# Weight halves kept in DRAM between passes and made beside the first MLP, and indexer scores over two PSUM tags

## The chip, the cores and the metric

One core of a Trainium2 chip runs the whole program. The metric is device time in microseconds (us), from the start of an execution to its end; lower is better. The engines are TensorE (PE, matmuls; PEld its weight loads), VectorE (DVE), ScalarE (ACT), GpSimd (POOL) and SyncE (SP), which here issues the DMA transfers.

## The reference, cut to what matters

Two layers over 1024 tokens of width 1024, in float32:

```python
for i in range(2):
    y = _even_mixer(h, ...) if i == 0 else _odd_mixer(h, positions, ...)
    h = _layer_norm(DN_ALPHA * h + y, ln1_g[i], ln1_b[i])
    u = square(relu(h @ mlp_w1[i])) @ mlp_w2[i]            # 1024 -> 4096 -> 1024
    h = _layer_norm(DN_ALPHA * h + u, ln2_g[i], ln2_b[i])
    h = h + sigmoid(h @ ple_gate_w[i]) * (p[i] @ ple_w[i])
```

The even mixer projects h with one matrix into an mLSTM (chunks of 64, a causal convolution on q and k) and into sparse attention with a compressed, a selected and a windowed branch. The odd mixer projects h to cq (512), ckv (256), a rope key and an indexer key, and then selects keys for each query:

```python
qi  = rope(cq @ w_iq)                                       # 8 indexer heads of 64
isc = einsum('bqh,bqhs->bqs', wi, relu(einsum('bqhd,bsd->bqhs', qi, ki)))
isc = where(causal, isc, NEG);  _, idx = lax.top_k(isc, 256)
q_abs = einsum('bthd,chd->bthc', (cq @ w_qb)[..., :128], w_uk)
o = masked softmax attention over the 256 selected (ckv, k_rope);  o = o @ w_uv, then @ w_out
```

## The kernel before, in words

A float32 product is made of three matmuls of reduced type (fp32r): each operand is split into a high half, hi, which is the value rounded to the reduced type, and a low half, lo = value - hi, and the kernel adds hi·hi, hi·lo and lo·hi in PSUM (L135, L138, L139 in `mm3`). Every weight tile therefore goes through `wload`: a DMA brings the raw 128x1024 floats into a buffer `wraw` (two of them), ACT writes hi into a buffer `wsp` (four of them, 128 x 2 x 1024; L115), and lo is written by DVE in one instruction (L122) or, where the flag `pool_lo` is set, by POOL in pieces of 256 columns (L120). Projections come as `lin_t` (tokens on the output's partitions) or `lin_f` (features).

The order is written out by hand with generators that are advanced in turn; a scheduler then orders the instructions of each engine, and waits are on buffers (a tile is handed on when its last reader is done). Each engine works in its own order, so an instruction that waits holds all behind it; all DMAs named here are issued in order on SP.

The stages, by the trace's clock:

- 0 to 690 us: the even mixer, in two halves of 512 tokens (the second from about 330 us). Each half reads the same 16 weight tiles for a-branch q/k, v and o (e_aqk, e_av, e_ao) in `mlstm_proj_steps`, with `pool_lo` set. `qk` (L429) is the convolution, on DVE; L743 to L806 are sparse attention.
- 690 to 1440 us: output projection and the first layer's MLP, `mlp`: eight chunks; in each, two passes of w1 (hidden, L858, L859, split by L94 and L95) and two passes of w2, in which DVE adds each of eight PSUM tiles to the residual H (L869).
- 1440 to 1540 us: the gate (ple).
- 1540 to 2170 us: the odd mixer. First kv, cq and the indexer keys of each half of the tokens; then `index_q` (rope products on POOL at L1063, a copy on POOL at L1143), and `idx(c, h)`, which for each query block c and head h makes scores in PSUM tag "s" (two banks; L1160), applies relu on ACT into a `w` buffer (L1163) and accumulates on DVE (L1165). The selection is a search with counts: comparisons L1398 on ACT and L1400 on DVE, and 128x2 bookkeeping L1394, L1402, L1403 on DVE, several blocks in turn. It shares the stretch of about 1680 to 1920 us with projections of the queries. `pool_lo` is set here from L1296 on.
- 2170 to 3044 us: second output projection, second MLP, gate and output.

`names1`, `presplit`, `wget` and `wkeep` do not exist before. `w2()` hands out activation buffers of 128x512, six of them, which the MLP's hidden pass and `idx` use.

Of the kernel before, what the change touches and what calls it, by code (L numbers as in the profile page):

```python
# [8 lines left out]
F32 = mybir.dt.float32  # L9
F32R = mybir.dt.float32r  # L10
BF16 = mybir.dt.bfloat16
I32 = mybir.dt.int32
AF = mybir.ActivationFunctionType
# [4 lines left out]
P = 128  # L18
# [29 lines left out]
class Kern:  # L48
    def __init__(self, tc, ins, out, dbg=None):
        self.tc = tc  # L50
        self.nc = tc.nc
        self.i = ins
        self.out = out
        self.dbg = dbg or {}
        self.uid = 0
        self.pool_lo = False
        self.pp = {}

    def nm(self, s):
# [42 lines left out]
    def wload(self, src, after=None, u=False):  # L102

        nc = self.nc
# [16 lines left out]
        else:  # L121
            nc.vector.tensor_sub(sp[1], raw[:, :n], sp[0].bitcast(F32))  # L122
        return sp

    def order(self, later, earlier):
# [250 lines left out]
    def mlstm_proj_init(self):  # L376
# [10 lines left out]
        self.halo = self.sm([P, 8, 3], tag="halo", bufs=1)  # L387

    def mlstm_proj_steps(self, hT, half):
        nc, i, an, cw = self.nc, self.i, self.an, self.cw  # L390

        def tok(name, n):
            def f():
                wch = [self.wload(i[name][n, k]) for k in range(2)]
                s = slice(n * 256, n * 256 + 256)
# [15 lines left out]
        def feat(grp):  # L411
            def f():
                wch = [self.wload(i["e_aqk"][grp, k]) for k in range(2)]
                for j in range(2):
# [394 lines left out]
    def tail(self, L, yT, wo, res, stop):  # L809
# [31 lines left out]
        return self.mlp(L, h1T, H, stop)  # L841

    def mlp(self, L, h1T, H, stop):
        nc, i = self.nc, self.i
        hv = self.hview(h1T)
        g2, b2 = self.row_bcast(i["ln2_g"][L]), self.row_bcast(i["ln2_b"][L])
        w1, w2 = i["mlp_w1"], i["mlp_w2"]
        h2T = [None, None]
        for ch in range(8):
            hid = [[None, None] for _ in range(4)]  # L850
# [20 lines left out]
            if ch < 7:  # L871
                for n in range(2):
                    wch = [self.wload(w2[L, ch, n, k]) for k in range(2)]
                    for mb in range(NB):
                        out(mb, n, wch)
            else:
                wch = [[self.wload(w2[L, ch, n, k]) for k in range(2)] for n in range(2)]
                for mb in range(NB):
# [11 lines left out]
    def ple_p(self, L, alloc, stage):  # L890

        nc, i = self.nc, self.i
        self.pp[L] = pd = self.dram([NB, P, 1024], F32, "pp")
        wp = [self.wload(i["ple_w"][L, n, 0], after=self.gate) for n in range(2)]
        for m2 in range(4):
# [171 lines left out]
    def mixer1(self, h3T, stop):  # L1067
# [62 lines left out]
        def index_q(half):  # L1130
            s = slice(half * 512, half * 512 + 512)
            for wg in range(2):
                wch = [self.wload(i["o_wiq"][wg])]
                for j in range(2):
# [16 lines left out]
        def idx(c, h):  # L1151
# [4 lines left out]
            for a in range(0, W, 512):  # L1156
                b = min(a + 512, W)
                ps = self.ps("s")
                for hl in range(2):
# [12 lines left out]
        def q_nope(wg):  # L1172
            wch = [self.wload(i["o_wqn"][wg])]
            for j in range(2):
# [7 lines left out]
        def q_rope(wg):  # L1182
            wch = [self.wload(i["o_wqr"][wg])]
            for j in range(2):
# [45 lines left out]
        def first():  # L1230
            W["k"] = [self.wload(i["o_wuk"][k], after=self.gate) for k in range(2)]
            W["v"] = [self.wload(i["o_wuv"][k], after=self.gate) for k in range(2)]
            self.mark = {}
# [61 lines left out]

        self.pool_lo = True  # L1296
        wch = [self.wload(i["o_wkv"][k]) for k in range(4)]
        for mb in range(4):
            part_kv(wch, mb)
        spare = self.u([P, 2, 1056], F32R, s="wsp", tag="mask")  # L1300
        wch = [self.wload(i["o_wcq"][k], u=spare if k == 3 else False) for k in range(4)]
        for mb in range(4):
# [12 lines left out]
        self.mt = self.u([P, 4224], BF16, s="mask", tag="mask")  # L1315
        wch = [self.wload(i["o_wkv"][k]) for k in range(4)]
        for mb in range(4, NB):
# [283 lines left out]
```

## Time and profile before

| | before |
|---|---|
| median of 3 runs | 3045.24 us (3043.98 to 3045.65) |
| the profiled execution | 3045.55 us, of which the span is 3043.8 us |
| mean granted TensorE clock | 0.983 |
| PE busy | 2917.3 us (96%) |
| DVE / ACT / POOL busy | 1658.0 / 1125.6 / 575.3 us |
| L120 on POOL | 248 instructions, 191.8 us |
| L115 on ACT | 217 instructions, 227.1 us |
| DMA | 280.83 MB, 92 GB/s over the span |

The span runs from the first to the last instruction; the execution is 1.75 us longer. A busy share is the time in which an engine had an instruction running, whether that instruction computed or was held inside by something else, so a longer mean of one form is as telling as the sum.

### The profile page before, as it was taken

Reading aid. Unit: us, or ns where it says so; the run is one execution under the profiler, and the core shown is the slowest. Engines: PE = TensorE matmul, PEld = TensorE weight load, DVE = VectorE, ACT = ScalarE, POOL = GpSimd, SP = SyncE. Lnnn points to the kernel's source line nnn. Section 1 sums busy time; section 2 is a strip of 40 time slices with the busy share of each in tenths; the row PEclk is TensorE's granted clock in tenths of the full one; section 3 lists DMA queues with packets and bytes.
Section 4 is the critical chain, followed back from the end, with each engine's and each line's share of the span. In section 5 each row is a group of like instructions: output and inputs, shape, how many; then the busy total and the mean of one; then the engine's idle time right before and its main releaser. Section 6 shows DMA issues by size and latency. Waiting matters only on the chain.

```text
span 3043.8 us, 39175 instructions
## 1 busy us (share of the span) xinstructions
PE 2917.3 (96%) x14583; PEld 2445.5 (80%) x14583; DVE 1658.0 (54%) x3808; ACT 1125.6 (37%) x2136; POOL 575.3 (19%) x681
## 2 busy tenths in 40 slices
PE   9999899989999999999999787899899999999999
PEld 8889787877888888888887466789788888888887
DVE  3587578765433333335557999966453333333372
ACT  3356655642222111213334668655232122222131
POOL 0254344312000000001343333221020000000032
PEclk9999999999999999999999899999999999999999
DMA  6642533343111111111321135654501111111122
GB/s 198 187 125 77 168 100 95 117 126 124 56 42 56 42 56 42 56 42 51 124 91 36 35 109 216 231 177 134 190 32 49 48 49 49 49 49 49 49 83 84
DMA packets 136751, 280.83 MB, mean 92 GB/s; under 512 B 14321, under 2 KB 64369, under 8 KB 136305
## 3 DMA queue, kind: packets, MB, share of 16 engines
q1 hardware_dynamic: 136560, 278.34, 28.3%
q8 instruction: 115, 1.88, 0.3%
q14 instruction: 76, 0.61, 0.1%
HBM read 209.08 MB, written 69.21 MB: 91 GB/s over the span
## 4 chain that ended last, share of the span: by engine, by line
PE 80%; DVE 11%; ACT 3%; issue 3%; DMA 3%; POOL 0%; SPq 0%; POOLq 0%; ACTq 0%; DVEq 0%
PE psmm L135 22%; PE psmm L138 22%; PE psmm L139 22%; PE psx L782 2%; PE pss L743 1%; PE psx L772 1%; PE psx L183 1%; DVE PT L95 1%; PE psx L1489 1%; DVE mask L1400 1%; DVE isc L1165 1%; DVE qk L429 1%; DVE ks L1394 1%; DVE PP L745 1%; DVE ks L1403 1%
## 5 line engine op out<-in xcount | busy, mean ns | idle before, releaser
L115 ACT ACTIVATE wsp<-wraw 128x1024 fp32r<-128x1024 f32 (+2 forms) x217 | 227.1, 1047 | 631.8 <-PE psmm L139 589.1
L135 PE MATMUL psmm<-wsp,hid 128*128 128x512 f32 x1024 | 399.1, 390 | 1.3 <-DVE pw L171 1.3
L138 PE MATMUL psmm<-h1T,wsp 128*128 128x512 f32 x1024 | 399.0, 390 | 0.2
L135 PE MATMUL psmm<-h1T,wsp 128*128 128x512 f32 x1024 | 398.2, 389 | 0.6 <-ACT h1T L94 0.6
L139 PE MATMUL psmm<-wsp,hid 128*128 128x512 f32 x1024 | 398.5, 389 | 0.0
L138 PE MATMUL psmm<-wsp,hid 128*128 128x512 f32 x1024 | 398.4, 389 | 0.0
L139 PE MATMUL psmm<-h1T,wsp 128*128 128x512 f32 x1024 | 398.2, 389 | 0.0
L869 DVE TENSOR_TENSOR H<-psmm,H 128x512 f32<-128x512 f32 x224 | 154.3, 689 | 296.6 <-PE psmm L139 296.5
L172 POOL TENSOR_TENSOR brs<-pw,mhalf 128x1 f32<-128x1 f32 x32 | 25.6, 799 | 1456.5 <-DVE pw L171 1398.9
L859 DVE SCALAR_TENSOR_TENSOR w<-psmm,w 128x512 f32<-128x512 f32 x128 | 88.6, 692 | 340.3 <-ACT w L858 340.3
L122 DVE TENSOR_TENSOR wsp<-wraw,wsp 128x1024 fp32r<-128x1024 f32 (+1 forms) x155 | 192.2, 1240 | 140.0 <-ACT wsp L115 139.6
L120 POOL TENSOR_TENSOR wsp<-wraw,wsp 128x256 fp32r<-128x256 f32 x248 | 191.8, 805 | 207.5 <-ACT wsp L115 196.1
L135 PEld LDWEIGHTS psmm<-wsp,hid 128*128 128x128 f32 x1024 | 192.2, 188 | 41.4 <-DVE pw L171 1.7
L135 PEld LDWEIGHTS psmm<-h1T,wsp 128*128 128x128 f32 x1024 | 192.1, 188 | 40.8 <-ACT h1T L94 1.1
L138 PEld LDWEIGHTS psmm<-h1T,wsp 128*128 128x128 f32 x1024 | 192.2, 188 | 40.6 <-DVE h1T L95 0.8
L139 PEld LDWEIGHTS psmm<-wsp,hid 128*128 128x128 f32 x1024 | 192.2, 188 | 40.0
L138 PEld LDWEIGHTS psmm<-wsp,hid 128*128 128x128 f32 x1024 | 192.2, 188 | 39.7
L139 PEld LDWEIGHTS psmm<-h1T,wsp 128*128 128x128 f32 x1024 | 192.2, 188 | 39.6
L858 ACT ACTIVATE w<-psmm 128x512 f32<-128x512 f32 x128 | 76.6, 598 | 395.1 <-PE psmm L139 395.1
L95 DVE TENSOR_TENSOR PT<-psx,PT 128x512 fp32r<-128x512 f32 (+4 forms) x272 | 154.8, 582 | 72.1 <-ACT PT L94 71.3
L94 ACT ACTIVATE PT<-psx 128x512 fp32r<-128x512 f32 (+4 forms) x272 | 135.2, 512 | 144.4 <-PE psx L772 77.1
L95 DVE TENSOR_TENSOR hid<-w,hid 128x512 fp32r<-128x512 f32 x128 | 88.4, 691 | 64.3 <-ACT hid L94 64.3
(475 smaller groups left out, 6287.0 us busy)
## 6 DMA issues: line engine op xcount, KB each, us to landing
wraw<-mlp_w SPq DMA_DIRECT2D x128, 512.0 KB, 3.6
wraw<-e_aqk SPq DMA_DIRECT2D x16, 512.0 KB, 4.3
pp<-pst SPq DMA_DIRECT2D x16, 512.0 KB, 2.7
wraw<-ple_gate_w SPq DMA_DIRECT2D x16, 512.0 KB, 3.7
pp<-pp SPq DMA_DIRECT2D x16, 512.0 KB, 3.9
qn<-stg SPq DMA_DIRECT2D x16, 512.0 KB, 2.9
yT<-od SPq DMA_DIRECT2D x16, 512.0 KB, 6.3
x<-x_t SPq DMA_DIRECT2D x8, 512.0 KB, 9.3
```

The costliest lines, as they stand in the source:

```text
L94: r = nc.scalar.activation(hi, src, AF.Copy)
L95: nc.vector.tensor_sub(lo, src, hi.bitcast(F32))
L115: nc.scalar.activation(sp[0], raw[:, :n], AF.Copy)
L120: nc.gpsimd.tensor_sub(sp[1][:, c], raw[:, c], sp[0][:, c].bitcast(F32))
L122: nc.vector.tensor_sub(sp[1], raw[:, :n], sp[0].bitcast(F32))
L135: m = nc.tensor.matmul(ps, wh, xh, start=(k == 0), stop=False)
L138: nc.tensor.matmul(ps, wh, xl, start=False, stop=False)
L139: nc.tensor.matmul(ps, wl, xh, start=False, stop=(k == n - 1))
L782: nc.tensor.matmul(pv[:, pr * 256:pr * 256 + 256], V[br - 1][:, k0 // 128 + t0 + t, :], PT[:, hl, t * 256:t * 256 + 256], start=False, sto ...
L858: nc.scalar.activation(r, ps, AF.Relu)
L859: nc.vector.scalar_tensor_tensor(out=r, in0=ps, scalar=0.0, in1=r, op0=ALU.max, op1=ALU.mult)
L869: nc.vector.tensor_add(hs, ps, hs)
```

## The change

Three edits. (1) `wkeep`: in the first half of the even mixer, each of the 16 split tiles is also stored to DRAM (hi and lo, 512 KB each); the second half loads hi and lo as one transfer of 1 MB straight into `wsp`. (2) `presplit` and `names1`: in the w2 passes of the first MLP, 22 weight tiles of the odd mixer and of the second gate are brought in pieces of at most 512 columns into a pair of `w2` buffers, split by ACT and DVE (lo in place), and stored to DRAM; one piece after every second output tile, 44 pieces. `wget` then loads the split tile where `wload` stood, and `pool_lo` is no longer set in the odd mixer. (3) `idx` takes the PSUM tags "s" (two banks) and "x" (four banks) in turn by head.

```diff
+    def presplit(self, names):
...
+                lo, hi = (self.w2(dt=F32R)[:, :b - a] for _ in range(2))
+                raw = lo.bitcast(F32)
+                self.load(raw, src[:, a:b])
+                nc.scalar.activation(hi, raw, AF.Copy)
+                nc.vector.tensor_sub(lo, raw, hi.bitcast(F32))
+                self.store(d[:, 0, a:b], hi.bitcast(F32))
+                self.store(d[:, 1, a:b], lo.bitcast(F32))
+                yield
...
+    def wget(self, key, n=1024, after=None, into=None):
+
+        if into == "raw":
+            t = [self.pwr.tile([P, 1024], F32R, tag="wraw", name=self.nm("wraw"))[:, :n] for _ in range(2)]
+            for k in range(2):
+                self.load(t[k].bitcast(F32), self.wd[key][:, k, :n], after)
+            return t
+        t = into if into is not None else self.pws.tile([P, 2, 1024], F32R, tag="wsp", name=self.nm("wsp"))
+        self.load(t[:, :, :n].bitcast(F32), self.wd[key][:, :, :n], after)
+        return [t[:, 0, :n], t[:, 1, :n]]
...
+    def wkeep(self, name, g, k, half):
+
+        if half == 0:
+            sp = self.wload(self.i[name][g, k])
+            d = self.wd[name, g, k] = self.dram([P, 2, 1024], F32, "wd")
+            for hl in range(2):
+                self.store(d[:, hl], sp[hl].bitcast(F32))
+            return sp
+        t = self.pws.tile([P, 2, 1024], F32R, tag="wsp", name=self.nm("wsp"))
+        self.load(t.bitcast(F32), self.wd[name, g, k])
+        return [t[:, 0], t[:, 1]]
...
-                wch = [self.wload(i[name][n, k]) for k in range(2)]
+                wch = [self.wkeep(name, n, k, half) for k in range(2)]
...
+        pre = self.presplit(self.names1() if L == 0 else ())
...
                         out(mb, n, wch)
+                        if mb % 2:
+                            next(pre, None)
...
-                wch = [self.wload(i["o_wiq"][wg])]
+                wch = [self.wget(("wiq", wg))]
...
-                ps = self.ps("s")
+                ps = self.ps(("s", "x")[h % 2])
...
-        self.pool_lo = True
-        wch = [self.wload(i["o_wkv"][k]) for k in range(4)]
+        wch = [self.wget(("wkv", k), 784, into=None if k else "raw") for k in range(4)]
```

The other calls of `wload` in the odd mixer (o_wcq, o_wqn, o_wqr, o_wuk, o_wuv, and ple_w of the second layer) become `wget` in the same way. In the changed file the same lines stand a little lower: L82 is L83, L95 is L96, L122 is L123, L869 is L918, L1063 and L1064 are L1119 and L1120, L1143 is L1199; L138 is there the `tensor_sub` of `presplit`, and L86 its stores.

The order of POOL at the end of the second `index_q` and the start of the queries' rope products (L1063, L1064), before:

```order
L1143 TENSOR_TENSOR qi_14007<-w_2349_14899,qi_14007 64x512
L120 TENSOR_TENSOR wsp_14939<-wraw_14937,wsp_14939 128x256 x4
L120 TENSOR_TENSOR wsp_14947<-wraw_14945,wsp_14947 128x256 x4
L120 TENSOR_TENSOR wsp_15558<-wraw_15556,wsp_15558 128x256 x4
L120 TENSOR_TENSOR wsp_15706<-wraw_15704,wsp_15706 128x256 x4
L120 TENSOR_TENSOR wsp_15854<-wraw_15852,wsp_15854 128x256 x4
L120 TENSOR_TENSOR wsp_15970<-wraw_15968,wsp_15970 128x256 x4
L1063 TENSOR_TENSOR w_2534_15577<-w_2534_15577,tab_15485 128x512
L1064 TENSOR_TENSOR w_2534_15577<-w_2534_15577,w_2536_15581 128x512
```

And with the change:

```order
L1199 TENSOR_TENSOR qi_14231<-w_2445_15089,qi_14231 64x512
L1119 TENSOR_TENSOR w_2627_15749<-w_2627_15749,tab_15663 128x512
L1120 TENSOR_TENSOR w_2627_15749<-w_2627_15749,w_2629_15753 128x512
L1119 TENSOR_TENSOR w_2632_15784<-w_2632_15784,tab_15663 128x512
L1120 TENSOR_TENSOR w_2632_15784<-w_2632_15784,w_2634_15788 128x512
```

The 24 low-half pieces between the two are gone, and POOL goes from the indexer's queries straight to the rope products.

SP's order at the start of the odd mixer, the loads of the weights for cq, the indexer queries and kv, before:

```order
L107 DMA wraw_13681<-o_wcq 128x1024
L107 DMA wraw_13914<-o_wiq 128x1024
L107 DMA wraw_13972<-o_wiq 128x1024
L107 DMA wraw_14316<-o_wkv 128x784
L107 DMA wraw_14324<-o_wkv 128x784
```

And with the change, where `wd` is the DRAM copy of a split tile:

```order
L83 DMA wraw_14540<-wd_8595 128x784
L83 DMA wraw_14541<-wd_8595 128x784
L83 DMA wsp_13919<-wd_9238 128x2048
L83 DMA wsp_13921<-wd_9319 128x2048
L83 DMA wsp_14150<-wd_9739 128x2048
L83 DMA wsp_14202<-wd_9810 128x2048
L83 DMA wsp_14544<-wd_8666 128x2x784
```

The loads that went to a `wraw` buffer, ahead of a split, now go to the `wsp` buffer from which PE reads, with twice the bytes; the second set of kv weights moved its first tile ahead of them, into the two `wraw` buffers.

DVE's order in a w2 pass of the first MLP (`H_n` are the eight residual tiles, L122 the low half of an MLP weight), before:

```order
L869 TENSOR_TENSOR H_7601<-psmm_9127,H_7601 128x512
L869 TENSOR_TENSOR H_7602<-psmm_9141,H_7602 128x512
L869 TENSOR_TENSOR H_7603<-psmm_9155,H_7603 128x512
L869 TENSOR_TENSOR H_7604<-psmm_9169,H_7604 128x512
L869 TENSOR_TENSOR H_7605<-psmm_9183,H_7605 128x512
L869 TENSOR_TENSOR H_7606<-psmm_9197,H_7606 128x512
```

And with the change:

```order
L918 TENSOR_TENSOR H_7553<-psmm_9139,H_7553 128x512
L138 TENSOR_TENSOR w_1609_9168<-w_1609_9168,w_1610_9169 128x512
L918 TENSOR_TENSOR H_7554<-psmm_9153,H_7554 128x512
L138 TENSOR_TENSOR w_1613_9203<-w_1613_9203,w_1614_9204 128x512
L918 TENSOR_TENSOR H_7555<-psmm_9175,H_7555 128x512
L138 TENSOR_TENSOR w_1618_9239<-w_1618_9239,w_1619_9240 128x512
L918 TENSOR_TENSOR H_7556<-psmm_9189,H_7556 128x512
L138 TENSOR_TENSOR w_1622_9274<-w_1622_9274,w_1623_9275 128x512
```

All eight pieces of a chunk come in the first of its two w2 passes, one behind almost every addition to H.

## Rows read from the trace of the kernel before

**Rows 1.** Windows by stage: bounds, length, busy of each engine, clock, DMA.

```profile
core 0: us, PE busy (x) PEld busy (x) DVE busy (x) ACT busy (x) POOL busy (x), PEclk, DMA share, GB/s
...
330.00:690.00 360.00, 330.86 (x2102) 288.82 (x2101) 254.57 (x781) 195.80 (x486) 127.43 (x186) 0.95 0.41 123
690.00:1440.00 750.00, 749.21 (x3341) 620.17 (x3341) 298.89 (x413) 170.11 (x226) 34.25 (x22) 1.00 0.17 54
...
1680.00:1920.00 240.00, 187.08 (x776) 140.11 (x774) 229.16 (x687) 172.87 (x339) 83.76 (x92) 0.90 0.39 137
```

**Rows 2.** The same windows for L120 alone, POOL's low halves of weights.

```profile
330.00:690.00 360.00, 50.98 (x64) 0.95 0.41 123
...
1680.00:1920.00 240.00, 44.29 (x56) 0.90 0.39 137
```

**Rows 3.** Timeline of POOL, then of DVE, from 1723.9 us.

```profile
1723.93 7.55 POOL L120 TENSOR_TENSOR wsp<-wraw,wsp 128x256 fp32r<-128x256 f32 x8 [2.44 <-issue]
...
1724.13 0.69 DVE L1402 TENSOR_TENSOR ks<-ks 128x2 int32<-128x2 f32 x1
1724.74 1.31 DVE L1165 SCALAR_TENSOR_TENSOR isc<-w,WI,isc 128x512 f32<-128x512 f32 x1
1725.98 0.68 DVE L1403 SCALAR_TENSOR_TENSOR ks<-ks 128x2 int32<-128x2 int32 x1
1726.58 1.30 DVE L1165 SCALAR_TENSOR_TENSOR isc<-w,WI,isc 128x512 f32<-128x512 f32 x1
1727.80 0.68 DVE L1394 TENSOR_SCALAR ks<-ks 128x2 int32<-128x2 int32 x1
1728.40 1.29 DVE L1165 SCALAR_TENSOR_TENSOR isc<-w,WI,isc 128x512 f32<-128x512 f32 x1
```

**Rows 4.** Groups by form on DVE, 1680 to 1920 us.

```profile
L1165 DVE SCALAR_TENSOR_TENSOR isc<-w,WI,isc 128x512 f32<-128x512 f32 x35 | 28.4, 816 | 0.6 <-ACT w L1163 0.6
L1403 DVE SCALAR_TENSOR_TENSOR ks<-ks 128x2 int32<-128x2 int32 x76 | 22.2, 296 | 0.4
L1394 DVE TENSOR_SCALAR ks<-ks 128x2 int32<-128x2 int32 x76 | 21.6, 286 | 0.5
L1402 DVE TENSOR_TENSOR ks<-ks 128x2 int32<-128x2 f32 x76 | 16.6, 219 | 5.2 <-ACT junk L1398 3.5 <-ACT mask L1398 1.2
```

**Rows 5.** Single lines on DVE, same stretch: ns minimum/median/maximum.

```profile
L1165 DVE SCALAR_TENSOR_TENSOR isc<-w,WI,isc x56: 340/744/1310, 1718.9 to 1795.2; 128x512 f32<-128x512 f32 x35, 128x384 f32<-128x384 f32 x7, 128x256 f32<-128x256 f32 x7, 128x128 f32<-128x128 f32 x7
...
L1403 DVE SCALAR_TENSOR_TENSOR ks<-ks x76: 121/156/1254, 1683.5 to 1916.7; 128x2 int32<-128x2 int32 x76
L1394 DVE TENSOR_SCALAR ks<-ks x76: 149/168/1249, 1684.4 to 1917.5; 128x2 int32<-128x2 int32 x76
```

**Rows 6.** Waits of PE, 1680 to 1920 us: total, times, longest.

```profile
PE pss L1160 <- ACT w L1163: 15.7, 18, 3.0
```

**Rows 7.** Waits of PE, 1540 to 1680 us.

```profile
PE psmm L135 <- ACT sc L1105: 2.5, 1, 2.5
```

**Rows 8.** Timeline of ACT and PE at the first half's indexer queries.

```profile
1619.00 1.06 ACT L115 ACTIVATE wsp<-wraw 128x1024 fp32r<-128x1024 f32 x1
...
1620.11 0.50 PE L135 MATMUL psmm<-cqT,wsp 128*128 128x512 f32 x1 [0.33 <-ACT wsp L115]
```

**Rows 9.** DMA issues: count, KB each, median us to landing.

```profile
wraw<-mlp_w SPq DMA_DIRECT2D x128, 512.0 KB, 3.6
...
h<-H SPq DMA_DIRECT2D x16, 256.0 KB, 2.5
w<-h SPq DMA_DIRECT2D x16, 256.0 KB, 5.8
...
w<-e_w SPq DMA_DIRECT2D x2, 1024.0 KB, 6.8
```

**Rows 10.** Line L429 on DVE, 330 to 690 us.

```profile
L429 DVE SCALAR_TENSOR_TENSOR qk<-raw,cw,qk x24: 734/1064/1307, 458.1 to 541.7; 128x512 f32<-128x512 f32 x24
```

**Rows 11.** Timeline of DVE in a w2 pass of the first MLP.

```profile
926.40 0.69 DVE L869 TENSOR_TENSOR H<-psmm,H 128x512 f32<-128x512 f32 x1 [2.03 <-PE psmm L139]
```

More of the change, by code (lines that the diff above doesn't have):

```diff
@@ L57, in __init__ @@
         self.pp = {}
+        self.wd = {}
     def nm(self, s):
@@ L123, in wload @@
         return sp
+    def presplit(self, names):
+        nc = self.nc
+        for key, src in names:
+            n = src.shape[1]
+            self.wd[key] = d = self.dram([P, 2, 1024], F32, "wd")
+            for a in range(0, n, 512):
+                b = min(a + 512, n)
+                lo, hi = (self.w2(dt=F32R)[:, :b - a] for _ in range(2))
[15 more added lines that the diff above has]
+        return [t[:, 0, :n], t[:, 1, :n]]
     def order(self, later, earlier):
@@ L412, in f @@
             def f():
-                wch = [self.wload(i["e_aqk"][grp, k]) for k in range(2)]
+                wch = [self.wkeep("e_aqk", grp, k, half) for k in range(2)]
                 for j in range(2):
@@ L841, in tail, with names1 @@
         return self.mlp(L, h1T, H, stop)
+    def names1(self):
+        i = self.i
+        r = [(("wkv", k), i["o_wkv"][k]) for k in range(4)] + [(("wcq", k), i["o_wcq"][k]) for k in range(4)]
+        r += [(("wiq", k), i["o_wiq"][k]) for k in range(2)] + [(("ple", k), i["ple_w"][1, k, 0]) for k in range(2)]
+        r += [(("wqr", k), i["o_wqr"][k]) for k in range(2)] + [(("wqn", k), i["o_wqn"][k]) for k in range(4)]
+        return r + [(("wuk", k), i["o_wuk"][k]) for k in range(2)] + [(("wuv", k), i["o_wuv"][k]) for k in range(2)]
     def mlp(self, L, h1T, H, stop):
@@ L875, in mlp @@
                         out(mb, n, wch)
-            else:
+                        if mb % 2:
+                            next(pre, None)
+            else:
+                for _ in pre:
+                    pass
                 wch = [[self.wload(w2[L, ch, n, k]) for k in range(2)] for n in range(2)]
@@ L893, in ple_p @@
         self.pp[L] = pd = self.dram([NB, P, 1024], F32, "pp")
-        wp = [self.wload(i["ple_w"][L, n, 0], after=self.gate) for n in range(2)]
+        if L == 1:
+            wp = [self.wget(("ple", n), after=self.gate) for n in range(2)]
+        else:
+            wp = [self.wload(i["ple_w"][L, n, 0], after=self.gate) for n in range(2)]
         for m2 in range(4):
@@ L1172, in q_nope @@
         def q_nope(wg):
-            wch = [self.wload(i["o_wqn"][wg])]
+            wch = [self.wget(("wqn", wg))]
             for j in range(2):
@@ L1182, in q_rope @@
         def q_rope(wg):
-            wch = [self.wload(i["o_wqr"][wg])]
+            wch = [self.wget(("wqr", wg))]
             for j in range(2):
@@ L1230, in first @@
         def first():
-            W["k"] = [self.wload(i["o_wuk"][k], after=self.gate) for k in range(2)]
-            W["v"] = [self.wload(i["o_wuv"][k], after=self.gate) for k in range(2)]
+            W["k"] = [self.wget(("wuk", k), after=self.gate) for k in range(2)]
+            W["v"] = [self.wget(("wuv", k), after=self.gate) for k in range(2)]
             self.mark = {}
@@ L1300, in mixer1 @@
         spare = self.u([P, 2, 1056], F32R, s="wsp", tag="mask")
-        wch = [self.wload(i["o_wcq"][k], u=spare if k == 3 else False) for k in range(4)]
+        wch = [self.wget(("wcq", k), into=(None, None, None, spare)[k]) for k in range(4)]
         for mb in range(4):
@@ L1315, in mixer1 @@
         self.mt = self.u([P, 4224], BF16, s="mask", tag="mask")
-        wch = [self.wload(i["o_wkv"][k]) for k in range(4)]
+        wch = [self.wget(("wkv", k), 784, into=None if k else "raw") for k in range(4)]
         for mb in range(4, NB):
```

## The prediction

> **What bounds the kernel now.** I read the busy table first: PE is busy for 2917.3 us of a span of 3043.8, so 126.5 us is all that the change can win while PE's own work stays as it is. Then the windows by stage, to see where that idle time lies [rows 1]. In the first MLP there is none (749.21 busy of 750.00): what is put beside that MLP on other engines costs nothing as long as PE is not made to wait. The second half of the even mixer has 29.1 us of it (360.00 - 330.86), the stretch of the indexer and the selection 52.9 (240.00 - 187.08). In that last stretch DVE is busy for 229.16 of 240.00 us, 95%: DVE sets its length, at a clock of 0.90.
>
> Next, whether those 229 us are DVE's own work. The timeline shows eight L120 pieces on POOL from 1723.93, 7.55 us long, and beside them 128x512 accumulations of 1.29 to 1.31 us and 128x2 operations of 0.68 and 0.69 [rows 3]. Their medians in the whole stretch are 0.744, 0.156 and 0.168 [rows 5]. So DVE operations that read from SBUF are held while POOL works, and the means by form are far above the medians [rows 4].
>
> **DVE freed in the selection (-16).** 56 L120 leave this stretch, 44.29 us of POOL [rows 2]; POOL's order in the section on the change shows the 24 of them between the indexer's queries and the rope products. Excess of mean over median in rows 4, with L1402 at the median of L1403 as the same 128x2 size: (816-744) x35 = 2.5, (296-156) x76 = 10.6, (286-168) x76 = 9.0, (219-156) x76 = 4.8 us, together 26.9. All of POOL's 83.76 us may cause that [rows 1]; L120's share by time is 44.29/83.76, so 14.2 us. That is the lower bound. The upper one is from rows 3: from 1724.13 to 1729.69, 5.56 us, the six rows cost 1.67 us (three accumulations) and 1.57 us (three small ones, with L1402 at 0.156) above their medians, 0.58 us for each us of L120; over 44.29 us, 25.8 us. I take the middle, 20. Of what DVE is given I let 0.8 reach the end: DVE is nearly full, but the search passes through ACT in each round and PE waits 15.7 us for ACT's relu [rows 6]. That is -16; ends -26 (all of the upper) and -9 (0.6 of the lower).
>
> This row also bears on a rule of the Trainium skill, "SBUF — State Buffer", section "🔬 SBUF: two separate sides": VectorE and GpSimd share a port pair as an exclusive lock that is held for a whole instruction, against VectorE operations with two SBUF inputs or in a two-port mode. By that every us of L120 would be lost to such operations; the trace agrees with the kind of operation, and shows 0.58 us for each us. The full price is a rival below.
>
> **Scores over six banks instead of two (-2).** PE waits 15.7 us in 18 times for the relu that empties an "s" bank [rows 6]. More banks let PE run ahead, but the accumulation on DVE behind ACT stays, so little of it is time at the end: -2, ends -5 (a third of those waits) and 0.
>
> **Start of the odd mixer (+1).** The split of a tile is replaced by its load into the buffer that PE reads. At the first half's queries ACT made hi from 1619.00 to 1620.06 and PE began at 1620.11, 1.1 us after the buffer came free [rows 8], since the raw floats already lay in `wraw`. Now 1 MB comes only after the release: the nearest rows say 6.8 us for 1 MB, 3.6 for 512 KB [rows 9], so 2.5 to 5.7 us later; I take 4 for this place. On the other side ACT loses its splits, and a wait of 2.5 us for ACT goes with them [rows 7]; I allow 3 for all of ACT's relief. +1, ends -3 and +6. SP's order shows the cause of the loss: each load waits for a `wsp` buffer, and what is behind it on SP waits too.
>
> **Second half of the even mixer (-6).** 64 L120, 50.98 us, and 16 L115 leave [rows 2]. The convolution shows what POOL costs there: 24 instructions of 1064 ns median against 734 at least [rows 10], 24 x 0.33 = 7.9 us of DVE. DVE is busy 71% (254.57/360.00), so not all of it counts, but `wraw` no longer carries these weights either. -6; ends 0 (DVE has the slack) and -15 (half of PE's 29.1 us of idle time).
>
> **First half (+1).** 32 stores of 512 KB, behind low halves on POOL, on SP's queue. No row has such a store. Lower bound 0, since the loads behind them run ahead of use; upper +3, one late load of 3.6 us [rows 9], less 0.6 of cover. I take +1.
>
> **First MLP (0).** 44 pieces: a load of 256 KB, an ACT copy, a DVE subtraction and two stores each. On DVE a piece stands behind each addition to H, and eight of these make one w2 pass. DVE idles 2.03 us before each addition of 0.69, so additions follow every 2.72 us [rows 11], and a subtraction of 128x512 of about that 0.69 fits in. What can be late is its data. SP issues the load of piece k+2 after the last store of piece k, so two pieces are in flight, and a piece takes (L + 0.53 + 0.69 + 0.69)/2, with landing L, half of ACT's 1.06 [rows 8], the subtraction and one addition ahead of it. That is 2.72 at L = 3.5. A 256 KB transfer lands after 2.5 us alone and 5.8 in a burst of 16 [rows 9]. The first is nearer: three transfers of 256 KB per 2.72 us are 289 GB/s, with the MLP's 54 in all 343; rows 1 have a share of 0.39 at 137, so 351 for a full share. Cover: if DVE's subtraction is late, the additions behind it are, and PE waits when both PSUM buffers are full, after about 2.0 us. 0, ends 0 and +10 (L = 4.5: eight pieces at 3.2 are 3.9 us late, less 2.0, over 5.5 passes).
>
> **Sum.** -16 -2 +1 -6 +1 +0 = -22 against the profiled execution of 3045.55 (1.75 beyond its span; 0.3 above the median of 3045.24): 3023.6, by the median 3023.2; I say 3024. The likeliest case's own range is 3010 to 3036.
>
> **Rivals.**
> - *The round binds, not DVE's sum.* If each search block waits for its own ACT and DVE rounds, DVE's freed time becomes idle time: -8 for the selection (half), 0 for the banks, -3 for the even mixer, +2 for the rest: 3036. Rows 4 speak for it, with 3.5 us of L1402 waiting for ACT; rows 1 speak against it, with 95% busy.
> - *Weight loads eat the gain.* In the odd mixer 36 loads have no raw copy ahead. Where a buffer's release is on the path, each costs up to 5.7 us; four such places cancel the 22: 3045, no change to be measured. For it: rows 8 are such a place. Against: elsewhere the raw loads too were issued well ahead.
> - *The pieces hold the MLP* (the other side). Above L = 3.5 us DVE's order puts the additions to H behind late pieces. It decides at L = 5.1: 3.5 us a piece, (8 x 0.78 - 2.0) x 5.5 = 23 us, all of the gain. At the 5.8 of rows 9 it is 3.86 a piece and 39 us: 3062. For it: the 343 GB/s against 351; against: 2.5 us for one transfer, and three in flight are no burst of 16.
> - *Every L120 is lost in full.* 44.29 x 0.8 = 35 in place of 16 in the selection and 12 in place of 6 in the even mixer, with -2, +1, +1: 2998. Rows 3 are against it with 0.58. It is what the rule quoted above from the Trainium skill would give.
>
> **How the numbers follow.** Forecast 0.56, round 0.13, loads 0.12, pieces 0.12, full price 0.07. A measurement of this kernel tells about 0.2%, 6 us, from no change: below 3039.2 is faster, above 3051.3 slower. Forecast, full price and nearly all of the round case are faster, 0.74; loads and the mild end of the pieces are the same, 0.15; the rest of the pieces and a worse load case are slower, 0.11. The range runs from 3004, short of the full price, to 3046, with the loads in it, and leaves out the pieces above it and the full price below.
>
> **What will show it.** In the changed profile: in the selection's stretch the four small and large DVE forms of rows 4 near the medians of rows 5, DVE's busy time there down by some 20 us and the stretch shorter by about as much; the L1160 wait on relu near zero; L429 near 0.75 us; at the first queries a wait of PE for a `wd` load of 3 to 6 us; in the first MLP PE still without idle time, the pieces' subtraction not longer than its addition, and landing of the 256 KB loads below 3.5 us. Wrong would make it: a PE wait for DVE in the MLP, PE waits for `wsp` loads at more than four places, or DVE idle time in the selection as large as what POOL's leaving gave it.

## The result, and the profile after

The changed kernel takes 3019.94 us (median of 4 runs, 3018.53 to 3023.94) against 3045.44 us for the kernel before in the same comparison: a ratio of 0.9915, interval 0.9898 to 0.9932, or 25.5 us less. A later comparison of the same two gave 3022.67 and 0.992 (0.9904 to 0.9935). The forecast was 3024, in a range of 3004 to 3046.

The total came out 4 us from the forecast, but parts of it were wrong by more than that, in opposite directions. To see it, both spans are cut at the same places of the program: the first addition of the output projection to H in the first layer (L826 before), the first sigmoid input of the first gate (L948), the last reading of a kv projection (L1100), the last transpose of attention weights (L1489), and the end. Windows of the kernel before, with the columns of [rows 1]:

```profile
0.00:686.30 686.30, 648.59 (x4039) 568.04 (x4039) 458.83 (x1329) 361.44 (x854) 234.89 (x353) 0.98 0.44 133
686.30:1471.60 785.30, 783.12 (x3496) 648.15 (x3497) 330.19 (x463) 182.56 (x241) 46.58 (x30) 1.00 0.18 59
1471.60:1680.60 209.00, 200.68 (x979) 168.75 (x977) 118.78 (x319) 83.89 (x163) 87.93 (x104) 0.99 0.24 75
1680.60:2157.60 477.00, 413.71 (x2181) 340.18 (x2182) 393.02 (x1202) 293.46 (x608) 132.58 (x148) 0.94 0.44 153
2157.60:3043.80 886.20, 871.16 (x3893) 720.36 (x3891) 357.15 (x497) 204.26 (x274) 73.31 (x48) 0.99 0.19 62
```

And of the changed kernel, cut at the same places:

```profile
0.00:674.40 674.40, 642.64 (x4039) 562.15 (x4039) 453.39 (x1328) 345.46 (x838) 184.42 (x289) 0.99 0.53 172
674.40:1474.70 800.30, 787.20 (x3495) 648.68 (x3496) 356.38 (x507) 208.40 (x284) 46.49 (x30) 1.00 0.31 99
1474.70:1682.50 207.80, 198.09 (x967) 168.16 (x966) 107.69 (x336) 68.63 (x143) 50.41 (x48) 0.99 0.31 107
1682.50:2131.50 449.00, 403.31 (x2198) 338.72 (x2196) 370.43 (x1186) 281.67 (x598) 90.13 (x91) 0.96 0.51 179
2131.50:3018.00 886.50, 870.61 (x3893) 720.04 (x3891) 357.24 (x497) 204.30 (x274) 73.31 (x48) 0.99 0.19 62
```

Even mixer -11.9 (the forecast's terms for it: -5), first MLP +15.0 (0), gate and head of the odd mixer -1.2 and selection with attention -28.0 (-17 for the two), tail +0.3: -25.8. PE's idle time (length less its busy time) went from 37.7 to 31.8, from 2.2 to 13.1, from 8.3 to 9.7, and from 63.3 to 45.7 us. So the first MLP, which had next to no idle time, has 13 us of it now. The longest of PE's waits in it, in total, times and longest:

```profile
PE psmm L164 <- DVE H L918: 8.0, 5, 2.7
PE psmm L164 <- DVE H L916: 2.6, 2, 1.9
```

They are for additions to H (L916 is that of the first chunk).

The rows that answer to those of before, in order. The four forms of [rows 4] on DVE, 1680 to 1920 us of the changed kernel:

```profile
L1221 DVE SCALAR_TENSOR_TENSOR isc<-w,WI,isc 128x512 f32<-128x512 f32 x35 | 25.4, 743 | 0.0
L1449 DVE TENSOR_SCALAR ks<-ks 128x2 int32<-128x2 int32 x80 | 17.6, 228 | 0.1
L1458 DVE SCALAR_TENSOR_TENSOR ks<-ks 128x2 int32<-128x2 int32 x80 | 15.9, 210 | 0.2
L1457 DVE TENSOR_TENSOR ks<-ks 128x2 int32<-128x2 f32 x80 | 14.4, 183 | 4.1 <-ACT junk L1453 1.9 <-ACT mask L1453 1.4
```

The accumulation is at its median, the small ones are nearer to theirs: what is left of POOL's work there still holds them. The trace shows it instruction by instruction: of the 80 operations of L1449, the 69 with no POOL instruction beside them take 171 ns at most and the 11 others 640 on average. Of the 76 of L1394 before, the 49 with none take 171 ns at most and the 27 others 508 on average. The convolution of [rows 10] and the waits of [rows 6] in the changed kernel:

```profile
L470 DVE SCALAR_TENSOR_TENSOR qk<-raw,cw,qk x24: 737/752/1276, 455.4 to 535.8; 128x512 f32<-128x512 f32 x24
```

```profile
PE psx L1216 <- ACT w L1219: 1.8, 2, 1.2
PE pss L1216 <- ACT w L1219: 1.2, 3, 0.5
```

Its median is 752 ns where it was 1064, and PE waits 3.0 us for the relu where it waited 15.7. The place of [rows 8], PE at the first half's indexer queries:

```profile
1627.22 0.50 PE L164 MATMUL psmm<-cqT,wsp 128*128 128x512 f32 x1 [2.92 <-DMA wsp<-wd]
```

PE waits 2.92 us for the split tile, where it waited 0.33. Such direct waits are at two places of the odd mixer:

```profile
PE psmm L164 <- DMA wsp<-wd: 4.0, 2, 2.9
```

DMA issues beside [rows 9], those of the first MLP's stretch and, last, of the odd mixer's:

```profile
w<-o_wcq SPq DMA_DIRECT2D x8, 256.0 KB, 3.8
w<-o_wqn SPq DMA_DIRECT2D x8, 256.0 KB, 4.0
...
w<-o_wiq SPq DMA_DIRECT2D x4, 256.0 KB, 4.4
```

```profile
wsp<-wd SPq DMA_DIRECT2D x20, 1024.0 KB, 6.9
```

Over all the pieces of 256 KB the medians are 3.5 to 4.4 us, by tensor. The 1 MB loads land after 6.9, as the 6.8 of [rows 9] said. Beside [rows 11], DVE in a first w2 pass of a chunk (888 to 914 us of the changed kernel), from its middle:

```profile
899.81 0.69 DVE L138 TENSOR_TENSOR w<-w,w 128x512 fp32r<-128x512 f32 x1 [2.93 <-ACT w L137]
900.42 0.68 DVE L918 TENSOR_TENSOR H<-psmm,H 128x512 f32<-128x512 f32 x1
901.84 0.69 DVE L138 TENSOR_TENSOR w<-w,w 128x512 fp32r<-128x512 f32 x1 [0.73 <-ACT w L137]
902.45 0.68 DVE L918 TENSOR_TENSOR H<-psmm,H 128x512 f32<-128x512 f32 x1
904.71 0.69 DVE L138 TENSOR_TENSOR w<-w,w 128x512 fp32r<-128x512 f32 x1 [1.58 <-ACT w L137]
907.93 0.69 DVE L138 TENSOR_TENSOR w<-w,w 128x512 fp32r<-128x512 f32 x1 [2.53 <-ACT w L137]
908.54 0.68 DVE L918 TENSOR_TENSOR H<-psmm,H 128x512 f32<-128x512 f32 x1
909.14 1.21 DVE L123 TENSOR_TENSOR wsp<-wraw,wsp 128x1024 fp32r<-128x1024 f32 x1
910.28 0.68 DVE L918 TENSOR_TENSOR H<-psmm,H 128x512 f32<-128x512 f32 x1
```

No addition (L918) has idle time before it that PE ended, as the one of [rows 11] had: each follows its predecessor at once, so it was ready earlier and was held. The idle time stands before the pieces (L138), and ACT's copy of the piece ended it. Between the additions at 902.45 and 908.54 lie 6.09 us and two pieces; PE needs 2.72 for one output tile.

### The profile page after: what moved, and what is told of

Its sections match the earlier page's. It is cut to its first block, busy times and chain, and to the rows that moved or that the text cites. A ratio compares the mean times of both kernels' runs of the same rounds, so it can differ in the third digit from the quotient of the medians.

```text
span 3018.0 us, 39426 instructions
## 1 busy us (share of the span) xinstructions
PE 2901.9 (96%) x14583; PEld 2437.8 (81%) x14583; DVE 1645.1 (55%) x3852; ACT 1108.4 (37%) x2136; POOL 444.8 (15%) x505
## 4 chain that ended last, share of the span: by engine, by line
PE 79%; DVE 9%; DMA 6%; ACT 3%; issue 2%; SPq 0%; POOL 0%; POOLq 0%; ACTq 0%; DVEq 0%
PE psmm L164 21%; PE psmm L167 21%; PE psmm L168 21%; PE psx L823 2%; PE psx L813 2%; PE pss L784 2%; PE psx L212 1%; PE psx L1544 1%; DVE PT L96 1%; PE pss L164 1%; PE pss L167 1%; PE pss L168 1%; DMA qn<-stg 1%; DMA w<-o_wqn 1%; DMA w<-o_wcq 1%
## 5 line engine op out<-in xcount | busy, mean ns | idle before, releaser
L116 ACT ACTIVATE wsp<-wraw 128x1024 fp32r<-128x1024 f32 (+1 forms) x173 | 182.1, 1053 | 512.2 <-PE psmm L168 477.1
L918 DVE TENSOR_TENSOR H<-psmm,H 128x512 f32<-128x512 f32 x224 | 154.0, 688 | 242.2 <-PE psmm L168 241.6
L123 DVE TENSOR_TENSOR wsp<-wraw,wsp 128x1024 fp32r<-128x1024 f32 (+1 forms) x155 | 192.2, 1240 | 132.6 <-ACT wsp L116 132.0
L167 PEld LDWEIGHTS psmm<-wsp,hid 128*128 128x128 f32 x1024 | 192.7, 188 | 39.4
L95 ACT ACTIVATE PT<-psx 128x512 fp32r<-128x512 f32 (+4 forms) x272 | 135.3, 513 | 145.7 <-PE psx L813 77.8
L96 DVE TENSOR_TENSOR PT<-psx,PT 128x512 fp32r<-128x512 f32 (+4 forms) x272 | 154.9, 581 | 59.7 <-ACT PT L95 58.2
L96 DVE TENSOR_TENSOR hid<-w,hid 128x512 fp32r<-128x512 f32 x128 | 88.3, 690 | 64.3 <-ACT hid L95 64.3
L804 POOL TENSOR_SCALAR PP<-PP,nst 128x640 f32<-128x640 f32 (+7 forms) x128 | 97.1, 772 | 91.4 <-DVE nst L847 48.8
```

The costliest lines, as they stand in the source:

```text
L95: r = nc.scalar.activation(hi, src, AF.Copy)
L96: nc.vector.tensor_sub(lo, src, hi.bitcast(F32))
L116: nc.scalar.activation(sp[0], raw[:, :n], AF.Copy)
L167: nc.tensor.matmul(ps, wh, xl, start=False, stop=False)
L804: nc.gpsimd.tensor_scalar(PP[h2][:, :WT], PP[h2][:, :WT], st[:, 3, h2:h2 + 1], 1.0, op0=ALU.mult, op1=ALU.mult)
L918: nc.vector.tensor_add(hs, ps, hs)
```

## The experiments

The table is read from such windows of each profile: us of length, and in brackets PE's idle time. The ratios are each to runs of the kernel before in the same comparison, whose medians were 3045.44 (changed), 3046.58 (keep, pieces, unused, no low halves), 3044.99 (banks, one tag, low halves on POOL, paced) and 3045.85 us (the rest).

| kernel | median, us | ratio (interval) | even mixer | first MLP | gate, head | selection, attention |
|---|---|---|---|---|---|---|
| before, profile 1 | 3045.24 | | 686.3 (37.7) | 785.3 (2.2) | 209.0 (8.3) | 477.0 (63.3) |
| before, profile 2 | | | 685.1 (38.8) | 785.7 (2.6) | 209.1 (8.5) | 479.1 (65.5) |
| changed, profile 1 | 3019.94 | 0.9915 (0.9898 to 0.9932) | 674.4 (31.8) | 800.3 (13.1) | 207.8 (9.7) | 449.0 (45.7) |
| changed, profile 2 | 3022.67 | 0.992 (0.9904 to 0.9935) | 674.7 (32.0) | 796.9 (11.5) | 208.4 (10.2) | 448.0 (44.0) |
| keep only | 3028.49 | 0.9937 (0.9924 to 0.9949) | 675.8 (30.8) | 784.8 (3.3) | 210.1 (9.1) | 469.5 (58.4) |
| pieces only | 3039.71 | 0.9973 (0.9962 to 0.9984) | 681.6 (38.3) | 798.2 (12.4) | 210.4 (8.7) | 452.9 (45.1) |
| pieces unused | 3062.34 | 1.0051 (1.0039 to 1.0064) | 687.8 (38.4) | 803.2 (14.2) | 210.3 (9.1) | 479.2 (63.4) |
| no low halves | 3019.89 | 0.991 (0.9896 to 0.9923) | 683.7 (39.4) | 785.5 (2.5) | 206.0 (6.4) | 456.5 (47.5) |
| banks only | 3033.81 | 0.9961 (0.9949 to 0.9974) | 681.7 (38.1) | 785.2 (3.7) | 207.3 (8.0) | 468.2 (63.0) |
| changed, one tag | 3031.69 | 0.9958 (0.9945 to 0.997) | 675.6 (33.9) | 802.0 (13.5) | 210.5 (9.9) | 451.2 (45.2) |
| low halves of pieces on POOL | 3014.06 | 0.9899 (0.9885 to 0.9912) | 669.8 (30.7) | 799.5 (12.6) | 208.5 (10.5) | 450.9 (44.9) |
| paced pieces | 3010.52 | 0.9887 (0.9872 to 0.9902) | 678.2 (32.1) | 791.1 (7.6) | 208.8 (10.6) | 450.6 (45.0) |
| paced, whole piece on POOL | 3004.77 | 0.9871 (0.9856 to 0.9886) | 675.1 (32.0) | 786.9 (3.8) | 207.1 (8.3) | 447.6 (43.2) |
| no low halves, two tags | 3006.21 | 0.9875 (0.9861 to 0.989) | 685.4 (36.9) | 785.4 (2.5) | 201.4 (5.5) | 444.5 (40.0) |

**Each edit alone, first the kept weights.** The calls of `wget` are `wload` again and `pool_lo` is set, no pieces are made, one PSUM tag:

```diff
-        pre = self.presplit(self.names1() if L == 0 else ())
+        pre = self.presplit(())
...
-                ps = self.ps(("s", "x")[h % 2])
+                ps = self.ps("s")
```

> Only the first edit (split weights of the even mixer kept in DRAM for its second half); odd mixer, indexer and MLP as before. Theory A (the trace of after: the output projection's first addition to the residual comes 11.9 us earlier, so the edit is worth twice what was forecast): 3033, with the even mixer 10 to 13 us shorter and nothing changed behind it. Theory B (the forecast's two terms, -6 and +1): 3040. Theory C (the gain in after has another source, such as the order of the program): 3043 to 3047.

Theory A by the even mixer: 10.5 us shorter, idle 30.8 in place of 37.7. The total gained more than A said, 18 us by the medians, because selection with attention, where no code changed, was 7.5 us shorter in this profile. That part isn't explained; A expected nothing to change there.

**The pieces alone** (one PSUM tag as above and `wkeep` is `wload`, but pieces and `wget` stay):

```diff
-                wch = [self.wkeep(name, n, k, half) for k in range(2)]
+                wch = [self.wload(self.i[name][n, k]) for k in range(2)]
```

> Only the second edit (pieces split beside the first MLP and loaded split by the odd mixer); even mixer as before, indexer on one PSUM tag. Theory A: the MLP loses 11 to 15 us, the odd mixer wins 25 to 29, so 3029 to 3034. Theory B (the indexer's second PSUM tag is what shortens the selection): the MLP's loss remains and the odd mixer wins under 10: 3045 to 3055.

The stages are as theory A has them: the MLP 12.9 us longer, selection with attention 24.1 shorter at 45.1 of idle time. The median of 3039.71 lies above A's range, though the profiled execution did not; runs of this kernel spread from 3030.68 to 3042.65. B falls: with one tag the gain in the selection is there.

**The pieces made and not used** (with the raw loads and POOL's low halves in the odd mixer, one PSUM tag, no kept weights):

```diff
-        wch = [self.wget(("wkv", k), 784, into=None if k else "raw") for k in range(4)]
+        self.pool_lo = True
+        wch = [self.wload(i["o_wkv"][k]) for k in range(4)]
```

> The pieces are split and stored beside the first MLP, but the odd mixer splits its raw weights as before, so that only the price of making the pieces is seen. Theory A (additions to the residual wait on VectorE behind late pieces): 3056 to 3060, with 10 to 12 us of TensorE waits for those additions in the first MLP. Theory B (the forecast: pieces are hidden): 3045 to 3049. Theory C (the loss in after belongs to the shifted start of the MLP or to the stage behind it): 3045, no TensorE waits in the MLP.

Theory A, 2 us above its range: 3062.34, 15.8 us above the before of its comparison (3046.58). Waits of PE in the first MLP of this run, in total, times and longest:

```profile
PE psmm L164 <- DVE H L918: 9.9, 6, 3.1
PE psmm L164 <- DVE H L916: 2.2, 2, 1.1
```

**No low halves in the odd mixer.** The kernel before, with the high half standing in for the low one there (that part of the computation is changed); matmuls, loads and ACT's splits stay:

```diff
+        if self.nolo:
+            return [sp[0], sp[0]]
         if self.pool_lo:
```

> The kernel before, but the odd mixer takes the high half of its weights in place of the low half too, so POOL makes no low halves there (this changes part of the computation); raw loads, ScalarE's splits, the PSUM tag and all matmuls stay. Theory A (VectorE is held by POOL's low halves): the selection's four VectorE forms fall to their medians and the whole is 16 to 26 us shorter: 3019 to 3029. Theory B (the gain is from ScalarE's splits gone, from loads or from PSUM): 3040 to 3046. Theory C (every us of POOL is lost on VectorE): 2998 to 3010.

Theory A: 26.7 us less by the medians, with POOL's low halves as the only work taken away. Of the four DVE forms the accumulation fell to its median (746 ns), the small ones to 205 to 248 ns, part of the way. The row of selection with attention:

```profile
1675.20:2131.70 456.50, 409.01 (x2197) 338.07 (x2195) 371.51 (x1181) 293.25 (x608) 84.28 (x91) 0.96 0.45 159
```

ACT is at 293.25, as before, so its relief is no part of this. Of DVE some instructions moved to the stage ahead (x1181 here in place of x1202), so both stages are taken together: 106.30 and 371.51 us of DVE in this run, 118.78 and 393.02 before, for 1522 and 1521 instructions. 34.0 us of DVE's time was being held. The low halves that are gone, 44.29 us of which are in [rows 2], are these of the kernel before in the two stages:

```profile
1471.60:2157.60 686.00, 82.30 (x112) 0.96 0.38 129
```

34.0 us of DVE for 82.3 us of POOL is 0.41 for each. Two other ways for the gain are PE waiting for the low halves themselves and work standing behind them on POOL. In the two stages of the kernel before, PE's own waits name no low half (one of its weight loads does, 3.4 us), and POOL only once, for a copy of the queries (L1143), 1.2 us; an indirect delay through POOL's queue isn't excluded.

**The banks alone, and the change without them.** One line in either direction:

```diff
-                ps = self.ps("s")
+                ps = self.ps(("s", "x")[h % 2])
```

> Only the third edit (indexer scores over two PSUM tags). Theory A (between the changed kernel and the run with the pieces alone, the stretch from the last kv projection to the first attention transpose differs by 11 us, 201 against 212, so the banks are worth about that): that stretch 217 us instead of 228, total 3034 to 3038. Theory B (the forecast, -2, because VectorE accumulates behind ScalarE anyway): 3042 to 3046. Theory C (banks help only once VectorE is not held by POOL): 3044 to 3046.

> The changed kernel with the indexer back on one PSUM tag. Theory A (banks worth about 11 us in the changed kernel): the stretch from the last kv projection to the first attention transpose 212 us, total 3029 to 3032. Theory B (the first two edits add up to what they gave alone, -18 and -7 by the ratio and median, and the banks are worth 2): 3020 to 3023.

In both comparisons two tags are worth about 10 us of the time (3033.81 against 3044.99; 3031.69 against 3019.94 or 3022.67: 9 to 12). The two kernels without low halves, with one tag above and two below, lie 13.7 us apart (3019.89 and 3006.21). Theory B falls in both, and C in the first: banks alone help. Where it comes from is less plain. In the first the idle time of selection with attention did not move (63.0 against 63.3); PE was busy for less. The window from 1680 to 1780 us, which holds most of the scores, of the kernel before, with banks only, with one tag in the changed kernel, and of the changed kernel:

```profile
1680.00:1780.00 100.00, 73.08 (x270) 50.05 (x269) 94.46 (x286) 65.62 (x142) 27.43 (x29) 0.86 0.17 58
```

```profile
1680.00:1780.00 100.00, 84.57 (x335) 61.25 (x334) 95.68 (x275) 72.21 (x154) 30.49 (x31) 0.92 0.24 83
```

```profile
1680.00:1780.00 100.00, 83.77 (x347) 60.42 (x346) 95.02 (x334) 69.21 (x158) 16.32 (x15) 0.93 0.29 106
```

```profile
1680.00:1780.00 100.00, 90.36 (x400) 68.64 (x399) 96.12 (x315) 76.49 (x168) 16.82 (x15) 0.97 0.38 137
```

DVE is full in all four. In the same 100 us PE did 270 matmuls before, 335 with banks, 347 in the changed kernel with one tag and 400 in the changed kernel (308 in the run without low halves); it had fewer gaps, and the granted clock was 0.86, 0.92, 0.93 and 0.97 of the 2.4 GHz level. PE's projections ran further ahead: between 1600 and 1830 us it did 60 of each of the three matmuls of projections of cq (`psmm<-cqT,wsp`) before, and 72 with banks only. The stretch of which A spoke, from the last kv projection to the first attention transpose, is 228.1 us before and 223.8 with banks only, where A said 217; it is 211.4 with one tag in the changed kernel, as A said, and 201.4 and 200.6 in the two profiles of the changed kernel. So two tags are worth 10 us there, but the rest of the stage gives most of it back: the stages differ by only 1 to 5 us each between one tag and two, and the 9 to 12 us of the total can't be put down to a place.

**The low halves of the pieces on POOL,** so that no addition stands behind a piece on DVE:

```diff
-                nc.vector.tensor_sub(lo, raw, hi.bitcast(F32))
+                nc.gpsimd.tensor_sub(lo, raw, hi.bitcast(F32))
```

> The changed kernel with the low half of each piece made on POOL instead of VectorE, so that no addition to the residual stands behind a piece; loads, ScalarE's copies and stores are the same. Theory A (the pieces cost the MLP its 15 us only through VectorE's order): no TensorE wait for the additions, the MLP at 785 to 787 us, total 3003 to 3008. Theory B (the cost comes from the DMA traffic or from the MLP weights' own loads behind the pieces on the queue): MLP still 795 to 800, total 3015 to 3020. Theory C (POOL holds VectorE's own low halves of the MLP weights in turn): in between.

Theory A falls: the MLP kept its 12.6 us of idle time (the total gained 5 to 8 us, each kernel against its own before; in the profile the even mixer is 4.6 us shorter, where the code did not change). B has the MLP's length right, but its cause doesn't follow yet, since PE still waited 8.1 us for the additions. ACT's timeline in this run shows a second queue, and DVE's row what it did:

```profile
901.99 0.63 ACT L137 ACTIVATE w<-w 128x512 fp32r<-128x512 f32 x1 [2.03 <-DMA w<-o_wcq]
902.53 1.04 ACT L116 ACTIVATE wsp<-wraw 128x1024 fp32r<-128x1024 f32 x1
905.46 0.63 ACT L137 ACTIVATE w<-w 128x512 fp32r<-128x512 f32 x1 [1.90 <-issue]
906.00 1.04 ACT L116 ACTIVATE wsp<-wraw 128x1024 fp32r<-128x1024 f32 x1
```

```profile
903.60 1.48 DVE L123 TENSOR_TENSOR wsp<-wraw,wsp 128x1024 fp32r<-128x1024 f32 x1 [3.94 <-ACT wsp L116]
905.00 0.68 DVE L918 TENSOR_TENSOR H<-psmm,H 128x512 f32<-128x512 f32 x1
```

ACT's split of the next MLP weight (L116) stands behind a piece's copy that waits for its DMA, DVE's low half of that weight (L123) behind the split, and the addition behind the low half. What theory C names is there too: L123 took 1.48 us beside POOL's work, where it took 1.21 above.

**Paced pieces.** Each load is placed behind the addition after which the code has it, in the scheduler's order alone:

```diff
-                self.load(raw, src[:, a:b])
+                self.load(raw, src[:, a:b], self.hadd)
...
-                    nc.vector.tensor_add(hs, ps, hs)
+                    self.hadd = nc.vector.tensor_add(hs, ps, hs)
```

> The changed kernel, with each piece's load placed behind the addition after which it is written, so that VectorE's order has one piece behind about every second addition in both w2 passes instead of one behind each in the first. Theory A (a piece takes 3 to 4 us where an addition comes every 2.72; at 5.44 it is in time, and one late piece is inside TensorE's two banks): MLP 785 to 789, total 3003 to 3010. Theory B (each piece costs the MLP some fixed time, 15 us over 44 pieces, wherever it stands): 3017 to 3021.

Between the two, nearer to A: the MLP at 791.1 with 7.6 of idle time, and 3010.52. What PE still waited for in its first MLP:

```profile
PE psmm L164 <- DVE H L918: 2.5, 4, 1.0
PE psmm L164 <- ACT wu L116: 2.4, 1, 2.4
```

**Paced, and both halves on POOL,** which has little else to do there:

```diff
-                nc.scalar.activation(hi, raw, AF.Copy)
-                nc.vector.tensor_sub(lo, raw, hi.bitcast(F32))
+                nc.gpsimd.tensor_copy(hi, raw)
+                nc.gpsimd.tensor_sub(lo, raw, hi.bitcast(F32))
```

> The paced version with both halves of each piece made on POOL, so that neither ScalarE's split of an MLP weight nor an addition on VectorE stands behind a piece. Theory A (the remaining 5 us of TensorE idle time in the paced run's MLP come from these two queues): MLP 785 to 787 us with 2 to 3 of idle time, total 3004 to 3008. Theory B (they come from MLP weights that arrive late behind the pieces' transfers): MLP still 789 to 792, total 3009 to 3012.

Theory A, though PE's idle time of 3.8 us is above its 2 to 3. The same pieces, transfers and bytes as in the paced kernel, on a queue behind which nothing of the MLP stands, cost it 1.6 us; B falls:

```profile
675.10:1462.00 786.90, 783.15 (x3495) 648.18 (x3496) 331.06 (x463) 182.51 (x241) 129.16 (x118) 1.00 0.31 101
```

At 3004.77 (ratio 0.9871) this version is faster than both kernels.

**What the loads of 1 MB cost.** No low halves, as above, with two tags (the same part of the computation is changed):

> The kernel before without low halves in the odd mixer (the high half stands in for them, so part of the computation is changed) and with the indexer over two PSUM tags; raw loads and ScalarE's splits stay. Against the changed kernel it lacks only the loads of 1 MB and ScalarE's relief. Theory A (those two are worth nothing together): selection with attention 447 to 451 us as in the changed kernel, total 3009 to 3013. Theory B (the loads of 1 MB cost several us there): 440 to 446. Theory C (ScalarE's relief is part of the gain): 452 to 457, as without the second tag.

Theory B by its range: selection with attention takes 444.5 us with 40.0 of idle time, against 448.0 to 449.0 and 44.0 to 45.7 in the changed kernel, and gate and head 201.4 against 207.8 to 208.4. In all that is 10 to 11 us in favour of raw loads and splits, though ACT's relief works the other way. But the same comparison with one tag shows nothing: the two stages together take 662.5 us without low halves, 661.7 in the changed kernel with one tag and 663.3 with the pieces only. So a price of the 1 MB loads beyond PE's direct waits of some 4 us isn't shown; gate and head alone differ by 4.6 us between the two runs without low halves.

**Once more, the two kernels.**

> The kernel before once more, for the profile alone, to see what one profile's stage lengths are worth: in the runs so far stages whose code did not change differ by up to 7.5 us (the even mixer 681.6 to 687.8, selection with attention 469.5 to 479.2) at idle times that agree within 5 us. Theory A (the granted clock differs from execution to execution; TensorE's idle time by stage is the steadier number): idle 38 in the even mixer, 2 in the MLP, 58 to 64 in selection with attention, lengths within 8 us of before. Theory B (the stage lengths are steady and small differences in them mean something): lengths within 1 us of before.

> The changed kernel once more, on one chip with the others and with a second profile. Theory A (gain as in the result): 3017 to 3023, idle time of TensorE 31 to 33 in the even mixer, 11 to 14 in the MLP, 44 to 47 in selection with attention. Theory B (the first comparison was helped by chance): 3024 to 3032.

The second profile of before is within 2.1 us of the first in every stage; its 65.5 us of idle time in selection with attention are just above A's 58 to 64. So the unchanged stages of other kernels, up to 8 us apart at much the same idle time, differ more than two profiles of one kernel; neither theory covers that. The second comparison of the changed kernel confirms the result, within A's range.

## Why the prediction was right, and where it was not

**DVE held by POOL's low halves (-16).** Right in mechanism, and nearly in size. The measured 0.41 us for each us of L120 makes 18.3 us of the 44.29 in the selection, where the forecast had 20 of DVE's time. Taking the low halves away alone cut PE's idle time there by 16 to 18 us, and the length by 20 to 23. The full price (rival four) needs DVE to lose all of POOL's time; it fell, at 0.41. The rule of the Trainium skill, "SBUF — State Buffer", section "🔬 SBUF: two separate sides", that of the two engines the one that starts first holds the shared ports for its whole instruction and the other is blocked, has its kind of conflict in these runs. It works in both directions, so it doesn't put a price on all of POOL's busy time, as rival four did: L120 itself took up to 1.37 us, at a median of 0.74, so part of its time is its own waiting.

**The round binds (rival one).** It said -8 for the selection. The freed time of DVE shortened it by more than twice that; it fell.

**Banks (-2).** The mechanism of the wait was right, 15.7 us to 3.0, and the size wrong: 9 to 14 us of the total in place of 2. The forecast looked at the accumulation behind the relu, which is still DVE's, and not at the projections that share PE with the scores: PE in order, stuck at a score, held those too. The matmul counts fit that; where the time goes in the end isn't shown.

**Start of the odd mixer (+1) and the loads rival.** PE's wait for the load came where it was put, 2.92 us in place of 0.33; that is 2.6 more, just inside the bounds of 2.5 to 5.7. The stage was 1 us shorter. The rival needed four places on the path at up to 5.7 us each, and PE waited directly at two, 4.0 us in all: it fell. Against a kernel with raw loads, two tags and no low halves the two stages are 10 to 11 us longer, with one tag they are level; so whether the loads cost more than these waits stays open.

**Even mixer (-6 and +1).** PE's idle time is 30.7 to 33.9 us in all profiles with kept weights and 36.9 to 39.4 in all others, some 6 us less, as forecast; the length fell by about 10.

**First MLP (0).** This is the step that failed: it measured +11 to +18, and the forecast's own sign of being wrong, a wait of PE for DVE in the MLP, came with 8.0 and 2.6 us. Its threshold was passed, as L is 3.5 to 4.4 us and not below 3.5. The 2.5 us that it took as the nearer row was that of a store (`h<-H` in [rows 9]); the loads of 256 KB in the kernel before landed after medians of 2.7 to 5.8. By the forecast's own formula L gives 2.7 to 3.2 us a piece, and would have cost 0 to 8 us. The rest is what the cover of 2.0 us left out. It was worked out from additions behind pieces on DVE; at the end of a pass two pieces stand between two additions, and the splits of the next MLP weights stand behind late pieces on ACT and in front of additions on DVE. The timeline of DVE above has both, the two pieces in a row and L123 between the last two additions; the rows of DVE's order ahead of the prediction stop short of that place. With the low halves on POOL DVE's share of it was gone and nothing was won. Paced, the pieces cost 6 us, and paced and wholly on POOL 1.6: what was left after the pacing was queues and not traffic. Of the part that the pacing won this isn't shown, since it moved the transfers too, and no run has the pieces on POOL without it. The pieces rival had the mechanism and the side, but more than all of the gain needed L of 5.1.

**Sum.** -22 against -25.5. The MLP's +15 was offset by some 8 us more from the banks than forecast and by lengths that fell further than idle time did, in the even mixer and the selection. That these errors nearly cancel is luck; the nearness of the total confirms none of the terms, and the first one rests on the run without low halves.

**Open.** Kept weights alone gained 18 us and pieces alone 7, but both together, with one tag, 13. The stages of the profiles do not add up to that, and PE's busy time for the same matmuls lies between 2899 and 2926 us. Why it differs that much from kernel to kernel isn't settled. Not tried: the split tile of the indexer queries loaded earlier, which the 2.92 us wait asks for.

## What to carry to other kernels

Background work that waits for a DMA belongs on an engine behind which nothing urgent stands. An engine with idle time hides its duration and not its lateness, and every queue that it passes counts, also those that feed the urgent instruction at second hand. When one engine is full, look for instructions of it whose mean is far above their median, and for what runs beside them. Read a stage by PE's idle time and by the busy time of the full engine; its length alone differed here by up to 8 us between kernels with the same code in that stage.

## What was not expected of the hardware

In the four windows of 100 us above, with the same DVE share (94 to 96 of 100 us), the granted clock was 0.86 of the 2.4 GHz level in the one where PE had the most gaps (73 us busy) and 0.97 in the one where it had the fewest (90). So where PE waited less, its clock was higher too; the runs show the two together and not which came first. A cast of 128x512 to the reduced type took POOL 0.61 us, as much as ACT's copy with 0.63:

```profile
L137 POOL CAST w<-w x44: 410/612/1010, 804.7 to 1256.4; 128x512 fp32r<-128x512 f32 x40, 128x272 fp32r<-128x272 f32 x4
```

```profile
L137 ACT ACTIVATE w<-w x44: 430/632/634, 798.9 to 1259.1; 128x512 fp32r<-128x512 f32 x40, 128x272 fp32r<-128x272 f32 x4
```
